# Sixteen projection blocks of a hybrid decoder layer as eight pairs of seven products each, with x of the SSD kept in memory by chunks

## The chip, the core and the metric

The kernel runs on one core of one Trainium2 chip. A core has a matrix engine (TensorE, PE), a vector engine (VectorE, DVE), a scalar engine (ScalarE, ACT), GpSimd (POOL) and a queue engine (SyncE, SP), and 16 DMA engines that all queues share. TensorE writes to PSUM (eight banks of 128 x 512 float32). The metric is the device time of one execution, in microseconds (us).

## The reference

One decoder layer over 1024 tokens of width 1024, in float32: a Mamba-2 scan (SSD) and a differential attention side by side, merged by gates, then a gated convolutional FFN. Cut to what the change touches:

```python
mod = silu(c) @ w_ada + b_ada                    # six rows of 1024: sh1, sc1, g1, sh2, sc2, g2
h = rms_norm(x, pre_norm1_w) * (1 + sc1) + sh1
z, xbc, dt_raw, q, k, v, gates = split(h @ w_in) # 1024, 1536, 16, 1024, 1024, 1024, 2048
xbc = silu(causal_dwconv(xbc, conv_w, conv_b))   # four taps
xs, B, C = split(xbc)                            # 1024, 256, 256
y_ssd = ssd(xs, dt, A, B, C)                     # chunks of 128 tokens; times silu(z), norm
q, k = partial_rope(q), partial_rope(k)          # 16 heads of 64, the first 16 dims of a head turn
merged = sigmoid(gate_ssd) * (y_ssd @ w_ssd_o) + sigmoid(gate_att) * (y_att @ w_attn_o)
x = x + g1 * rms_norm(merged @ w_out)
u = causal_dwconv(h2 @ w_up, ...)                # h2 from x, sh2, sc2
x = x + g2 * rms_norm((gelu(u_gate) * u_val) @ w_down)
```

## The kernel before

**Products in three parts.** A float32 operand is split into a high part, rounded to the fast matmul's precision, and the rest, low (`split`, lines 92 to 94: ScalarE makes hi, VectorE lo). A product is hi·hi + hi·lo + lo·hi (`mm3`, lines 112 to 117). A *block* is 128 columns of a weight against all tokens: two halves of 512 tokens, eight k tiles of 128, three matmuls each, so 48 matmuls of 128x512 (`block_half`). h is held transposed and split in `hT[k][half]`, k the tile of 128 channels.

**Storage.** Working tiles of 128 x 1024 float32 come from a list of slots (`SL.get`, `SL.put`): a tile that takes a slot waits for all that still read or write the tile before it. Weights come through `wraw` (three buffers), `whi` and `wlo` (four each). In PSUM `ps_mm` has two pairs of banks, `ps_wa` two single banks, `ps_wb` and `ps_wc` one each.

**Order.** Each engine works through one list in order. In a `tc.manual_schedule` stretch the engines named run in the order of the program; elsewhere, and for the others, a planner orders them by its own estimates. POOL's list is always the planner's. SP issues the loads and stores, in order, and waits at each for what it needs.

**Stages**, by TensorE:

1. x is normed, scaled and transposed; beside it the first gate block and xbc blocks 0 and 1.
2. Gate block 1, xbc blocks 2 to 11, gate block 2. After each xbc block comes its convolution, one ScalarE step and three on VectorE (line 443) out of PSUM, then silu; the results `xbcT[0..11]` stay in slots until the SSD is done. Beside it run the *ada sums*: 32 tiles of `w_ada` (512 KB each, four buffers `adas`) are scaled by c and summed on VectorE (`ada_sum`), eight to a row; `ada_row` (lines 389 to 404) adds the partitions with two matmuls, adds b_ada (in `brow`, loaded by POOL's queue) and stores the row (`rowd`) for later stages.
3. z, in three column groups of 346 to 348, eight token tiles each, with softplus and decays of the SSD beside it. Each tile is evicted by ScalarE and VectorE (lines 585, 586) to `ev` and stored. Here POOL makes the first six *down sums* (`down_sums`, lines 409 to 420): two loads of `w_down` (512 KB each), four subtractions of 128 x 512, two stores to `wtd`, for the FFN's down projection, which uses the same scheme of seven products as the change.
4. The SSD by chunks, with v beside it.
5. Gate blocks 3 to 7, with the other five down sums on POOL.
6. q and k: four blocks with rope (lines 911 to 915, POOL has one multiplication of it, line 913) and one more of each without (`w_q`, `w_k` block 2), stored by head in pieces (`store_qk`, 16 stores a rope block); beside it y of the SSD is turned (`turn_y`).
7. so: eight blocks y @ w_ssd_o, times the gates, to memory (`msd`). At blocks 2 and 3, `load_qk` fetches q and k of the first two heads.
8. Attention by heads, in which the rest of q and k is projected; its output product; out; the up projection; down.

The up projection (lines 1452 to 1454, from 1256.9 to 1685.3 us) already computes its 44 blocks as 22 pairs of seven products.

Of the kernel before, what the change touches and what calls it, by code (L numbers as in the profile page):

```python
# [61 lines left out]
def kernel(ctx: ExitStack, tc: tile.TileContext, a: dict, out: bass.AP, dbg=None):  # L62
# [94 lines left out]
    xhs = [SL.get(f"xh{i}", F32, (P, 2, HALF)) for i in range(2)]  # L157
    vev = SL.get("vev", F32, (P, 2, HALF))
# [72 lines left out]
    def make_h(k, half):  # L231
# [4 lines left out]
        xh = xhs[n_h // 2 % 2][:, n_h % 2, :]  # L236
# [85 lines left out]
    SL.put(junk, *adat, *acc0, *xts, *xhs)  # L322
# [30 lines left out]

    def gate_out(ps, half, dst):
# [4 lines left out]
    for half in range(2):  # L359
        gate_out(pg0[half], half, gsd[0])  # L360

    def gate_block(j):
        w = load_block(a["w_gate"][j], f"wgs{j}")
        for half in range(2):
            ps = ps_wa(f"gs{j}_{half}")
            block_half(ps, w, hT, half)
            gate_out(ps, half, gsd[j])

    gate_block(1)

    accr = [SL.get(f"accr{i}") for i in range(2)]
    adas = [SL.get(f"adas{i}") for i in range(4)]
    nrow = SL.get("nrow")

    def ada_load(u):
        r, k = divmod(u, KD)
        SP.dma_start(adas[u % 4], a["w_ada"][k * P : (k + 1) * P, (r + 2) * D : (r + 3) * D])

    def ada_sum(u):
        r, k = divmod(u, KD)
        acc = accr[r % 2]
        if k == 0:
            V.tensor_scalar(acc, adas[u % 4], scl[:, 0:1], None, op0=ALU.mult)
        else:
            V.scalar_tensor_tensor(acc, adas[u % 4], scl[:, k : k + 1], acc, op0=ALU.mult, op1=ALU.add)

    def ada_row(r):
        g, acc = r + 2, accr[r % 2]  # L390
        br, nr = brow[0:1, :], nrow[0:1, :]
        G.dma_start(br, a["b_ada"][0:1, g * D : (g + 1) * D])
        if g != 3:
            G.dma_start(nr, a["norms"][r : r + 1, :])
        for half in range(2):
            pr = (ps_wb, ps_wc)[half](f"adar{g}_{half}")
            hsl = slice(half * HALF, (half + 1) * HALF)
            T.matmul(pr, ones, acc[:, hsl], start=True, stop=True)
            V.tensor_tensor(br[:, hsl], pr[0:1, :], br[:, hsl], op=ALU.add)
        if g != 3:  # L400
            V.scalar_tensor_tensor(br, br, 1.0 if g == 4 else 0.0, nr, op0=ALU.add, op1=ALU.mult)
        if r == 0:
            V.tensor_scalar(br, br, 0.5, None, op0=ALU.mult)
        G.dma_start(rowd[r], br)

    brow = SL.get("brow")
# [14 lines left out]

    n_ada, rows_done = 0, 0


    cu = [SL.get(f"cu{i}") for i in range(2)]
    xbcT = []
    with tc.manual_schedule(engines={EN.PE}):
        for b in range(12):
            if b < 2:
                ps = px0[b]  # L430
                for u in (2 * b, 2 * b + 1):
                    ada_load(u)
            else:
                w = load_block(a["w_xbc"][b], f"wx{b}")
                ps = ps_mm(f"xbc{b}")
                for half in range(2):
                    block_half(ps[:, half, :], w, hT, half)
            pf = ps.rearrange("p h t -> p (h t)")
            u = cu[b % 2]
            cw = vec[:, V_CW + 4 * b : V_CW + 4 * b + 4]  # L440
            A.activation(u, pf, AF.Identity, scale=cw[:, 3:4], bias=vec[:, V_CB + b : V_CB + b + 1])
            for d in (1, 2, 3):
                V.scalar_tensor_tensor(u[:, d:], pf[:, : S - d], cw[:, 3 - d : 4 - d], u[:, d:], op0=ALU.mult, op1=ALU.add)
            o = SL.get(f"xbcT{b}")
            A.activation(o, u, AF.Silu)
            xbcT.append(o)
            if b >= 2:
                while rows_done < n_ada // KD:
                    ada_row(rows_done)
                    rows_done += 1  # L450
                for _ in range(4 if b in (5, 9) else 3):
                    ada_sum(n_ada)
                    if n_ada + 4 < 32:
                        ada_load(n_ada + 4)
                    n_ada += 1
        gate_block(2)
    ada_row(3)
    assert n_ada == 32 and rows_done == 3
    SL.put(*cu, *accr, *adas, nrow, brow)
    wdr = [SL.get_last(f"wdr{i}", F32, (P, 2, HALF)) for i in range(2)]  # L460
    wds = [SL.get_last(f"wds{i}", F32, (P, 2, HALF)) for i in range(2)]
    xsT, BT, CT = xbcT[:8], xbcT[8:10], xbcT[10:12]
    if dbg is not None and "xbcT" in dbg:
        for b in range(12):
            SP.dma_start(dbg["xbcT"][b], xbcT[b])
# [90 lines left out]
    with tc.manual_schedule(engines={EN.PE, EN.DVE, EN.Activation, EN.SP}):  # L556
        for t_, (c0, wdt) in enumerate(thirds):
            if t_ == 0:
                wz = []
                for kp in range(4):  # L560
                    wz.append(split_z(c0, wdt, kp, z_raw.pop(0)))
            else:
                wz = wz_next
# [1471 lines left out]
```

## Time and profile before

| | |
|---|---|
| median of 3 runs | 1907.18 us (1906.95 to 1908.35) |
| the profiled execution | 1905.24 us, its span 1903.5 us |
| granted TensorE clock | 0.999 |
| TensorE busy | 1860.1 us, 98% of the span |
| VectorE, ScalarE, POOL busy | 1205.6, 848.8, 213.0 us |
| moved by DMA | 309.48 MB, 163 GB/s in the mean |

A line of a group shows source line, engine, operation, output<-input, shapes and count, then busy time and mean ns of one, then the idle time of the engine ahead of it and what ended that. In the table by windows each row is a stretch of time with the busy time of each engine in it. L115 is line 115 of the kernel before; the kernel after has other line numbers.

### The profile page before, as it was taken

To read this page: it belongs to the slowest core of one execution; us is meant where nothing else is said; L and a number is where in the kernel's file an instruction comes from. 1 tells how busy PE (TensorE), PEld (TensorE's weight loads), DVE (VectorE), ACT (ScalarE), POOL (GpSimd) and SP (SyncE) were. 2 spreads that over 40 slices of the span, in tenths; PEclk is the share of its full clock that TensorE was granted. 3 is DMA by queue.
4 is the path that set the end of the run, shared out by engine and by line. 5 is a ranking of instruction groups with operands and counts; after the bars stand their busy time and mean duration, and the time that the engine had idled before them with its cause. 6 is when DMAs were issued, how large, how long until landed. Compare 5 with 4: busy or idle time off the path is not lost.

```text
span 1903.5 us, 24513 instructions
## 1 busy us (share of the span) xinstructions
PE 1860.1 (98%) x9128; PEld 1552.4 (82%) x9128; DVE 1205.6 (63%) x1815; ACT 848.8 (45%) x1628; POOL 213.0 (11%) x225
## 2 busy tenths in 40 slices
PE   6999999999999999999999999999999999999998
PEld 4788898888888888888888788888788888888886
DVE  6957344575235237767667465378888888876545
ACT  5522124464223115665656423465454545455532
POOL 0000253453351000000000010000000000000001
PEclk9999999999999999999999999999999999999999
DMA  9834374233766846565652666122323322378754
GB/s 306 268 115 152 129 246 153 72 117 128 257 198 146 265 153 181 150 189 159 164 164 84 218 221 219 45 78 89 127 100 108 114 100 94 108 224 302 249 152 159
DMA packets 135575, 309.48 MB, mean 163 GB/s; under 512 B 17056, under 2 KB 48416, under 8 KB 135456
## 3 DMA queue, kind: packets, MB, share of 16 engines
q1 hardware_dynamic: 127808, 281.65, 46.3%
q0 software_dynamic: 7648, 26.26, 4.0%
q8 instruction: 72, 1.18, 0.3%
q14 instruction: 47, 0.39, 0.1%
HBM read 218.97 MB, written 88.88 MB: 162 GB/s over the span
## 4 chain that ended last, share of the span: by engine, by line
PE 77%; DVE 9%; DMA 5%; ACT 5%; POOL 2%; issue 2%; SPq 1%; POOLq 0%; ACTq 0%; DVEq 0%
PE upx L1453 3%; PE upx L1452 3%; PE upx L1454 3%; PE o L1143 3%; PE xbc L115 2%; PE xbc L116 2%; PE xbc L117 2%; DMA wdr<-in_w_down 2%; PE dx L1816 2%; PE dx L1817 2%; PE dx L1815 2%; PE dy L1816 2%; PE dy L1817 2%; PE dy L1815 2%; PE v L667 2%
## 5 line engine op out<-in xcount | busy, mean ns | idle before, releaser
L1452 PE MATMUL upx<-t,wu_t 128*128 128x512 f32 x264 | 103.6, 392 | 1.8 <-DVE cv L1878 1.0
L1453 PE MATMUL upx<-t,wu_t 128*128 128x512 f32 x264 | 102.9, 390 | 0.2 <-DVE t L1570 0.2
L1454 PE MATMUL upx<-t,wu_t 128*128 128x512 f32 x264 | 102.8, 389 | 0.0
L1426 ACT ACTIVATE wu_t<-sab 128x512 fp32r<-128x512 f32 x57 | 34.2, 627 | 133.1 <-DVE sab L1443 133.1
L1131 ACT COPY aT<-at 128x512 f32<-128x512 f32 (+2 forms) x96 | 46.1, 480 | 102.8 <-PE at L1130 102.8
L1143 PEld LDWEIGHTS o<-vt,aT 128*128 128x128 f32 x576 | 74.6, 191 | 9.8 <-ACT aT L1131 5.8
L1143 PE MATMUL o<-vt,aT 128*128 128x128 f32 x576 | 80.9, 277 | 0.3
L94 DVE TENSOR_TENSOR g_lo<-gst,g_hi 128x1024 fp32r<-128x1024 f32 (+1 forms) x42 | 47.5, 1135 | 49.6 <-ACT g_hi L93 49.5
L142 POOL TENSOR_TENSOR rsf<-rsf,nhalf 128x1 f32<-128x1 f32 x8 | 5.6, 705 | 628.9 <-DVE rsf L141 626.1
L93 ACT ACTIVATE g_hi<-gst 128x1024 fp32r<-128x1024 f32 (+1 forms) x42 | 41.4, 988 | 64.3 <-DMA gst<-gld_s 35.3
L142 POOL TENSOR_TENSOR sqt<-sqt,nhalf 128x4 f32<-128x4 f32 x16 | 16.6, 1036 | 465.3 <-DVE sqt L141 465.3
L1104 DVE TENSOR_REDUCE nmx<-sc 128x1 f32<-128x640 f32 (+3 forms) x64 | 65.6, 1025 | 2.2
L1084 PE MATMUL sc<-kst,qst 128*128 128x512 f32 (+2 forms) x192 | 63.8, 340 | 0.0
L115 PE MATMUL xbc<-hT,wx_hi 128*128 128x512 f32 x160 | 63.5, 397 | 0.0
L1085 PE MATMUL sc<-klo,qst 128*128 128x512 f32 (+2 forms) x192 | 63.2, 346 | 0.0
L117 PE MATMUL xbc<-hT,wx_lo 128*128 128x512 f32 x160 | 62.3, 389 | 0.0
L116 PE MATMUL xbc<-hT,wx_hi 128*128 128x512 f32 x160 | 62.2, 389 | 0.0
L115 PE MATMUL z<-wz_hi,hT 128*128 128x346 f32 (+1 forms) x192 | 62.1, 323 | 0.0
L116 PE MATMUL z<-wz_lo,hT 128*128 128x346 f32 (+1 forms) x192 | 61.7, 322 | 0.0
L117 PE MATMUL z<-wz_hi,hT 128*128 128x346 f32 (+1 forms) x192 | 61.4, 320 | 0.0
L1452 PEld LDWEIGHTS upx<-t,wu_t 128*128 128x128 f32 x264 | 49.5, 188 | 14.5 <-DVE cv L1878 3.2
L1470 DVE SCALAR_TENSOR_TENSOR ug<-cg,vec,ug 128x1023 f32<-128x1023 f32 (+1 forms) x44 | 56.3, 1280 | 7.7 <-ACT ug L1469 6.7
(451 smaller groups left out, 5840.6 us busy)
## 6 DMA issues: line engine op xcount, KB each, us to landing
adas<-in_w_ada SPq DMA_DIRECT2D x32, 512.0 KB, 4.9
wdr<-in_w_down POOLq DMA_DIRECT2D x22, 512.0 KB, 6.8
wtd<-wds POOLq DMA_DIRECT2D x22, 512.0 KB, 4.3
wuf<-in_w_up SPq DMA_DIRECT2D x22, 512.0 KB, 3.5
gld_s<-gsum SPq DMA_DIRECT2D x22, 512.0 KB, 2.8
gst<-gld_s SPq DMA_DIRECT2D x20, 512.0 KB, 4.5
wdt_raw<-wtd SPq DMA_DIRECT2D x20, 512.0 KB, 4.8
wuv<-in_w_up SPq DMA_DIRECT2D x19, 512.0 KB, 3.5
```

The lines of the kernel that those rows point to most:

```text
L115: T.matmul(ps, lh, rh, start=(i == 0), stop=False)
L116: T.matmul(ps, lh, rl, start=False, stop=False)
L117: T.matmul(ps, ll, rh, start=False, stop=(i == n - 1))
L1084: T.matmul(sc[:, n0:n1], qs_[s][:, tsl], ks_[s][:, n0:n1], start=True, stop=False)
L1104: V.reduce_max(nmx[:, bq, s : s + 1], sc[:, :L], axis=AX.X, negate=True)
L1143: T.matmul(po_of[j, grp][:, qi, :], at[:, k, :], vt[j % 2][:, kt, :], start=(kt == 0), stop=(kt == i))
L1452: T.matmul(out_, wh, xh_, start=(k == 0 and first), stop=False, skip_group_check=not first)
L1453: T.matmul(out_, wh, xl_, start=False, stop=False, skip_group_check=not first)
L1454: T.matmul(out_, wl, xh_, start=False, stop=(k == end), skip_group_check=not first)
L1815: T.matmul(o, gh[:, kk, tsl], wh, start=(k == 0 and not more), stop=False, skip_group_check=more)
L1816: T.matmul(o, gh[:, kk, tsl], wl, start=False, stop=False, skip_group_check=more)
L1817: T.matmul(o, gl[:, kk, tsl], wh, start=False, stop=(k == KF - 1), skip_group_check=more)
```

## The change

Sixteen blocks are computed in pairs: gate blocks 4 with 5 and 6 with 7, block 2 of w_q with block 2 of w_k, and xbc blocks 2 with 3 to 10 with 11. Channels of h and tokens are each cut in half, so that h is a 2 by 2 matrix of quarters (b11, b12, b21, b22) and the two blocks' weights another; Strassen's scheme in Winograd's form gives the four results in seven products of half the depth (12 matmuls each) instead of eight. It takes four sums of quarters of h (t1 to t4, made once, split into hi and lo) and four sums of weights for each pair (`x_sum`), and the seven products are summed in three banks: X three times, Z and Y.

- Gate blocks 1 to 3 come first, as plain blocks; beside them VectorE and ScalarE make t1 to t4 from h in 32 bits (`hr`). The quarter b12 of `hT` goes to memory (`h12d`), gives up its slots, and is loaded again during the last pair.
- The eight pairs follow, in an order written by hand for all engines but POOL. `post` does what belongs to a pair's blocks (tanh and store, scale and store, convolution and silu) under the products of the next pair, out of SBUF (`cg`, `cv`) instead of PSUM.
- PSUM is laid out anew for pairs and z: four single banks (`ps_x`), X and Z of a pair in two of them by turns, Y in `ps_wa`.
- Ada sums: six in each of the pairs 2 and 3, four in pair 4, with two buffers; the other 16 in z, one a tile from tile 6 on, with four. The rows are finished at z's tiles 2, 5, 16 and 23.
- xbc blocks 0 to 7 (x of the SSD) are stored to memory by chunks (`xcd`) and loaded a chunk at a time, two ahead (`xch`), instead of staying in slots.
- The stage of gates 3 to 7 and the two q, k blocks without rope are gone; the four rope blocks share one pair of `hi`, `lo` tiles, and `turn_y` follows them four at a time. The five down sums of the gates' stage are at so's blocks 0 to 4, and `load_qk` of the first two heads at blocks 5 and 6.

```diff
+    order = (("b11", "X"), ("b21", "Z"), ("t2", "X"), ("t1", "Y"), ("t3", "X"), ("b22", "Y"), ("t4", "X"))
+    pairs = [("gs", 4, 5), ("gs", 6, 7), ("qk", 2, 2)] + [("xbc", b, b + 1) for b in range(2, 12, 2)]
...
+    def x_mms(m, p):
+        n, bk = order[p]
+        o, t = xbank[m][bk], xhl[m, p]
+        first = p in (0, 1, 3)
+        for k in range(KH):
+            wh, wl = t[:, 0, k, :], t[:, 1, k, :]
+            xh_, xl_ = HX[n][k][:, 0, :], HX[n][k][:, 1, :]
+            T.matmul(o, wh, xh_, start=(k == 0 and first), stop=False, skip_group_check=not first)
+            T.matmul(o, wh, xl_, start=False, stop=False, skip_group_check=not first)
+            T.matmul(o, wl, xh_, start=False, stop=(k == KH - 1), skip_group_check=not first)
...
+            for p in range(7):
+                if p == 3:
+                    bank["Y"] = ps_wa(f"xy{m}")
+                x_mms(m, p)
+                if p == 0:
+                    if m > 0:
+                        x_sum(m, 3)
+                    x_ahead(m, 3)
+                    if m > 0:
+                        A.copy(cgv[(m - 1) % 2][1][:, :HALF], xbank[m - 1]["X"])
+                elif p == 1:
+                    A.copy(ev_[:, 0, :], bank["X"])
...
+                elif p == 5:
+                    V.tensor_tensor(cv[:, HALF:], bank["X"], ev_[:, 0, :], op=ALU.add)
+                    x_sum(m + 1, 0)
+                    x_ahead(m, 8)
...
+                for st in steps_at[before].get(p, ()):
+                    post(m - 1, st)
+                if m in (1, 2) and p < 6 or m == 3 and p in (1, 3, 4, 5):
+                    ada_sum(m < 3 or p < 4)
...
+                    if p == 2:
+                        for k in range(KH):
+                            hT[k][1] = new_hl(f"b12_{k}")
+                            SP.dma_start(hT[k][1].rearrange("p h t -> p (h t)").bitcast(F32), h12d[k])
...
 # z, tile nz = 8 * t_ + i
+                if nz < 6:
+                    post(last_pair, nz)
+                if nz < 22:
+                    if nz >= 2 and n_ald < 20:
+                        ada_load()
+                    if nz >= 6:
+                        ada_sum()
+                if nz in (0, 3, 14, 18):
+                    row_load((0, 3, 14, 18).index(nz))
+                if nz in (2, 5, 16, 23):
+                    ada_row((2, 5, 16, 23).index(nz))
...
 # SSD
-            T.transpose(px[:, j * P : (j + 1) * P], xsT[4 * g + j][:, tok], ident)
+            T.transpose(px[:, j * P : (j + 1) * P], xch[c % 2][:, 4 * g + j, :], ident)
+        if g == 1 and c < 6:
+            SP.dma_start(xch[c % 2], xcd[:, c + 2])
...
-    for j in range(3, 8):
-        down_sums(n_dn)
-        n_dn += 1
-        w = load_block(a["w_gate"][j], f"wgs{j}")
-        ps = ps_mm(f"gs{j}")
...
 # so, block j
-            if j in (2, 3):
-                s = j - 2
+            if j < 5:
+                down_sums(n_dn)
+                n_dn += 1
+            elif j == 5:
+                SL.put(*wdr, *wds)
+                qst, kst, klo = [[[SL.get(f"{n}0_{s}", F32R) for s in range(2)]] for n in ("qst", "kst", "klo")]
+            if j in (5, 6):
+                s = j - 5
                 load_qk(s, qst[0][s], kst[0][s], klo[0][s])
```

More of the change, by code (lines that the diff above doesn't have):

```diff
@@ L377, in ada_load @@
[L377 to L394, printed above, removed]
-        for half in range(2):
[L396 to L404, printed above, removed]
@@ new lines, with x_load @@
+    xw, xhl, xbank = {}, {}, {}
+    x_loads = [(n, m) for m in range(len(pairs)) for n in "fv"]
+    def x_load():
+        if not x_loads:
+            return
+        n, m = x_loads.pop(0)
+        kind, i, j = pairs[m]
+        src = {"gs": ("w_gate", "w_gate"), "xbc": ("w_xbc", "w_xbc"), "qk": ("w_q", "w_k")}[kind]["fv".index(n)]
+        t = xw[n, m] = wp.tile([P, 2, KH, P], F32, tag="wraw", name=f"xw{n}{m}", bufs=3)
+        SP.dma_start(t.rearrange("p h k c -> p (h k c)"), a[src][(i, j)["fv".index(n)]])
@@ L420, in down_sums @@
             G.dma_start(wtd[("12", "34")[i]][:, k, :, :], wds[i])
[L422 to L465, printed above, removed]
     sm1 = SL.get("sm1", F32, (P, 8, 8, NH))
@@ L891 @@
     load_y(0)
-    qscale = {"w_q": 0.125, "w_k": 1.0}
     ropc = SL.get("ropc")
@@ L896 @@
     SP.dma_start(rops, a["rops"])
-    thl = [[SL.get(f"th{n}{i}", F32R) for n in ("hi", "lo")] for i in range(2)]
+    hi, lo = [SL.get(f"th{n}", F32R) for n in ("hi", "lo")]
     qf = SL.get("qf")
```

387 lines of the change are left out of this document (303 added, 84 removed).

## The prediction

> **What bounds the kernel now.** I read the page first, then the windows by stage, then the waits of each stage that the change touches, and last the order of the instructions on each engine in the two built programs.
>
> ```profile
> span 1903.5 us, 24513 instructions
> PE 1860.1 (98%) x9128; PEld 1552.4 (82%) x9128; DVE 1205.6 (63%) x1815; ACT 848.8 (45%) x1628; POOL 213.0 (11%) x225
> ```
> ```profile
> 88.30:214.80 126.50, 126.50 (x546) 102.14 (x545) 82.59 (x74) 34.76 (x35) 3.89 (x8) 1.00 0.38 123
> 214.80:307.60 92.80, 92.80 (x590) 92.42 (x589) 36.21 (x76) 21.28 (x42) 43.94 (x49) 1.00 0.69 236
> 487.00:540.00 53.00, 53.00 (x235) 43.89 (x234) 6.95 (x5) 10.17 (x15) 25.05 (x27) 1.00 0.73 258
> 601.40:693.50 92.10, 91.91 (x420) 75.12 (x419) 25.69 (x34) 14.97 (x19) 0.00 (x0) 1.00 0.69 221
> ```
>
> The columns of a window are its length, then the busy time of PE, PEld, DVE, ACT and POOL, the granted clock, the DMA share and GB/s. TensorE has no gap in xbc with gate 2 (first row), z (second), gates 3 to 7 (third) and the SSD output product, so (fourth). A matmul that goes is a gain, and a wait that comes is a loss in full. POOL was busy beside z and gates 3 to 7, and idle beside so. There the change moves things.
>
> **The products removed.** Eight pairs of blocks take 7 products of 12 matmuls, where two plain blocks take 96: 12 fewer a pair, 96 in all. Their price is the distance of starts, read where the same scheme runs already (the up projection), first and last of 16 starts:
>
> ```profile
> 1681.65 0.39 PE L1454 MATMUL upy<-b,wu_b 128*128 128x512 f32 x1
> ...
> 1685.05 0.39 PE L1454 MATMUL upx<-t,wu_t 128*128 128x512 f32 x1
> ```
>
> (1685.05 − 1681.65) / 15 = 0.227 us, so 96 of them are **−21.8 us**. A product is 2.72 us, a pair 19.0, a plain block of 48 is 10.9.
>
> **Do pairs run dense?** The up projection says nearly:
>
> ```profile
> 1256.90:1685.28 428.38, 425.08 (x1882) 349.50 (x1880) 361.40 (x480) 219.58 (x330) 1.47 (x2) 1.00 0.31 108
> L1452 PE MATMUL upx<-t,wu_t 128*128 128x512 f32 x264 | 103.6, 392 | 1.8 <-DVE cv L1878 1.0
> L1452 PE MATMUL upy<-b,wu_b 128*128 128x512 f32 x88 | 34.5, 392 | 1.3 <-ACT evs L1875 1.3
> ```
> ```profile
> L1878 DVE TENSOR_TENSOR cv<-upx,evs x20: 681/684/692, 1315.5 to 1681.0; 128x512 f32<-128x512 f32 x20
> L1470 DVE SCALAR_TENSOR_TENSOR ug<-cg,vec,ug 128x1023 f32<-128x1023 f32 (+1 forms) x44 | 56.3, 1280 | 7.7 <-ACT ug L1469 6.7
> ```
>
> Its 22 pairs waited 1.8 + 1.3 us, 0.14 a pair: eight pairs **+1.1**. VectorE has in an xbc pair what it has there, 14 steps of 0.684 and 6 convolution steps of 1.28: 17.3 of 19.0 us.
>
> In pairs 2 and 3 six, in pair 4 four ada sums take the convolutions' place or come on top, and each waits for its own load, with two buffers for four:
>
> ```profile
> adas<-in_w_ada SPq DMA_DIRECT2D x32, 512.0 KB, 4.9
> L387 DVE SCALAR_TENSOR_TENSOR accr<-adas,scl,accr 128x1024 f32<-128x1024 f32 x20 | 25.6, 1281 | 2.2 <-DMA adas<-in_w_ada 1.9
> ```
>
> A buffer is needed again two products (5.4 us) after the sum that frees it began; less 1.3 for that sum some 4.1 us are left, and the products' 0.7 or so of slack on VectorE. A load that lands in 4.9 costs nothing; six loads, two of weights and two stores in 19.0 us are 10 × 0.524 MB, 275 GB/s against 123 there now, so one of 6 us is likely and costs about 1.4 a pair, since the evacuations of the banks stand behind the waiting sum. I take **+2.0** (0 to 6).
>
> At the end of the last pair z's first tile takes the bank that ScalarE must still copy out, one copy with its signals:
>
> ```profile
> L1859 ACT COPY cv<-upx x19: 564/568/589, 1322.0 to 1666.7; 128x512 f32<-128x512 f32 x19
> ```
>
> **+0.8.** The tile's last weights and the reloaded quarter of h land before it by my count (0 to 3).
>
> **Z: a row that waits behind three down sums.** This is the largest unknown. The program order is that the second row of ada (b_ada, line 788 after) is loaded at tile 3 and added on VectorE at tile 5. In the built program POOL has that load behind the first TENSOR_TENSOR of the fourth down sum, and VectorE, in order, has the row's addition ahead of the eviction of tile 6 and of all four lo halves that tile 8 needs. So PE stops at tile 8 until POOL has got through three sums and a load.
>
> ```profile
> 225.57 1.28 POOL L415 TENSOR_TENSOR wds<-wdr 128x512 f32<-128x512 f32 x1 [5.25 <-DMA zd<-ev]
> ...
> 253.04 1.28 POOL L416 TENSOR_TENSOR wds<-wdr,wds 128x512 f32<-128x512 f32 x1 [1.01 <-DMA wdr<-in_w_down]
> ...
> 292.79 1.29 POOL L415 TENSOR_TENSOR wds<-wdr 128x512 f32<-128x512 f32 x1 [6.38 <-DMA wdr<-in_w_down]
> ```
> ```profile
> wdr<-in_w_down POOLq DMA_DIRECT2D x12, 512.0 KB, 7.2
> wtd<-wds POOLq DMA_DIRECT2D x12, 512.0 KB, 4.4
> DMA to landing us min/median/max: 3.8/7.2/8.5
> brow<-in_b_ada POOLq DMA_DIRECT2D x4, 4.0 KB, 3.7
> L586 DVE SCALAR_TENSOR_TENSOR ev<-ev,z 128x346 f32<-128x346 f32 x8 | 4.1, 513 | 11.1 <-ACT ev L585 7.0 <-DMA zd<-ev 4.0
> L94 DVE TENSOR_TENSOR wz_lo<-wz_raw,wz_hi 128x692 fp32r<-128x692 f32 x3 | 2.6, 880 | 0.7 <-ACT wz_hi L93 0.5
> L399 DVE TENSOR_TENSOR brow<-adar,brow x8: 668/669/672, 135.5 to 215.7; 1x512 f32<-1x512 f32 x8
> ```
>
> A sum takes POOL (292.79 − 225.57) / 5 = 13.4 us from start to start. Count from the end of the last pair. The first sum's second wdr load waits for the sixth weight split of that pair, about −9.5; with 0.5 to issue, 7.2 to land and three steps of 1.29 the sum ends at +2.1. The second ends 13.4 + 1.0 later (the row's two small loads are issued in it), the third another 13.4: 29.9. Two stores, a load and a store issued (about 1.6), 7.2 to land, 1.3 for the step: 39.5 or so; the row's load lands 3.7 later, 43.2. VectorE then has two additions (1.3), the eviction of tile 6 (0.7 with its dt part), an ada term (0.7 to 1.3) and the first lo half (0.9): 46.8. Tile 8 is due at 0.8 + 8 × 92.8/24 plus two ada rows on PE, each (126.5 − 11 × 10.9) / 4 = 1.7: 35.2. The stall is **+11.6**. With each of the four loads at 3.8 it is 0, at 8.5 it is 17.
>
> That DVE and POOL hold each other up is in the rows of the same stage:
>
> ```profile
> L505 DVE TENSOR_TENSOR sm<-sm,sm 128x128 f32<-128x128 f32 x6 | 1.8, 292 | 0.2
> L497 DVE TENSOR_TENSOR sm<-sm,sm 128x128 f32<-128x128 f32 x1 | 1.3, 1332 | 0.0
> ```
>
> The same form takes 0.29 us, and 1.33 where it started at 253.15 beside POOL's step above. The change brings 6 convolution steps and 16 ada sums into this stage. VectorE has 36.2 + 22 × 1.28 + three more rows (about 7), 71 us of 92.8, and by the measured 1.04 for each of POOL's 24 steps at most 25 more, which it can still hold. I add **+0.5** for the split at tile 15. The Trainium skill, SBUF — State Buffer, Who interferes with whom, says that a VectorE instruction with two SBUF inputs and a GpSimd instruction that reads SBUF block each other for a whole instruction; the trace agrees (1.33 against 0.29), and it speaks against moving two-input work beside the down sums.
>
> The granted clock is 1.00 in every window above. The Trainium skill, TensorE: Matmul & The Clock Gate, Why this matters for your kernels, lets the clock fall to half after idle gaps of some 3 us; by it the stall would cost, as an estimate, 2 us more. No stretch here shows that.
>
> The last ada row stands ahead of half of v's lo halves on VectorE: two additions and one step of 1.2, up to 2.5 us at the start of the SSD, where x comes from memory two chunks ahead and should not be late. **+1.0** (0 to 2.5).
>
> **Gates 3 to 7 and q2, k2 gone; five down sums into so.** The gates ran dense, so only the saving counted above is in them. They also hid five down sums:
>
> ```profile
> 511.22 1.30 POOL L415 TENSOR_TENSOR wds<-wdr 128x512 f32<-128x512 f32 x1 [8.04 <-DMA wdr<-in_w_down]
> ...
> 536.64 1.28 POOL L415 TENSOR_TENSOR wds<-wdr 128x512 f32<-128x512 f32 x1 [5.54 <-DMA wdr<-in_w_down]
> ```
> ```profile
> 599.77 0.42 SPq L864 DMA_DIRECT2D khd<-thhi  x1
> ...
> 602.09 0.42 SPq L865 DMA_DIRECT2D kld<-thlo  x1
> L912 DVE STREAM_SHUFFLE sw<-qf 128x1024 f32<-128x1024 f32 x4 | 5.3, 1334 | 0.0
> L914 DVE TENSOR_TENSOR sw<-sw,rops 128x1024 f32<-128x1024 f32 x4 | 10.3, 2570 | 0.0
> L915 DVE TENSOR_TENSOR qf<-qf,sw 128x1024 f32<-128x1024 f32 x4 | 4.9, 1217 | 8.1 <-POOL qf L913 8.0
> L93 ACT ACTIVATE wso_hi<-wso_raw 128x1024 fp32r<-128x1024 f32 x8 | 8.5, 1056 | 48.8 <-DMA wso_raw<-in_w_ssd_o 48.8
> L94 DVE TENSOR_TENSOR wso_lo<-wso_raw,wso_hi 128x1024 fp32r<-128x1024 f32 x8 | 9.8, 1223 | 21.2 <-ACT wso_hi L93 21.2
> wso_raw<-in_w_ssd_o SPq DMA_DIRECT2D x6, 512.0 KB, 5.0
> klo<-kld SPq DMA_DIRECT2D x4, 256.0 KB, 9.0
> ```
>
> Times now from the start of so: 4.7 us of turning y (92.1 − 8 × 10.9), then blocks of 10.9. q2 and k2 used to lie between the last rope block and so. Now the fourth rope block's steps stand on VectorE behind so's first eviction (15.6 + 0.7): shuffle, multiply, add, hi, lo, 1.3 + 2.6 + 1.2 + 1.1 + 1.2, to 23.7. Its 16 stores leave SP 0.46 apart, 7.4 us, and three more issues come before the load of block 3's weights is out at 32.5: landed 37.5, hi and lo 39.8, due 37.4. **+2.7** with the eviction's load beside it (0 to 5).
>
> POOL's first sum there needs the slots of those stores, so its second load starts at about 33.5: landed 40.5, done 44.4. Four more at 12.9 (between the 12.7 of the rows above and 13.4) end at 96. SP, in order, has the loads of k's low half for the heads 0 in slots that the last sum frees, and so waits from about 80 to 96; behind it stand the other loads of the first two heads, two stores, v and the weights of w_k3. The last of k low needs the store of the sum (96 + 4.4) and 9.0 to land: 110. PE ends so at 94.6, has q products of later heads to fill in (14 groups of three matmuls, 9.5 us), 104, and waits **+6.0**. A sum ending at 90 costs nothing; each us later costs about one.
>
> **The sum.** −21.8 + 1.1 + 2.0 + 0.8 + 11.6 + 0.5 + 1.0 + 2.7 + 6.0 = +3.9. The profiled execution took 1905.24 (span 1903.5 and 1.74 outside it), 1.94 less than the median of 1907.18: its like would be 1909.1, and the median **1911**. 0.2%, about what a measurement can tell from no change, is 3.8 us.
>
> **The rivals.** *POOL's period is short* (faster). Both stalls hang on how long a down sum takes. At 11 us each, as where loads land in 5, the row comes two periods of 2.4 and two loads of 2.2 sooner, 9 us, and the last sum of so ends at 86: −9 and −6, 1911 − 15 = 1896; at 12 us about 1902. For it: the two periods in gates 3 to 7 were 12.7, and z's loads landed in as little as 3.8. Against: DMA has more to carry in the new z (16 ada loads). Periods half a microsecond shorter than I take make 4 us, that is, before and after alike.
>
> *POOL's period is long* (slower). Z's 236 GB/s are 21.9 MB in 92.8 us; 16 ada loads of 0.524 make them 326 GB/s, and five sums with four such transfers each take so from 221 to 335. If a sum then takes 16 us, the two periods ahead of the row add 5 and the four in so add 12: 1911 + 17 = 1928. For it: these rates, and the lock on VectorE; against: POOL's loads have a queue of their own.
>
> *All waits hidden:* −21.8 + 1.1 + 0.8 + 0.5 + 1.0 leaves 1889. It needs POOL to run the row's load earlier than its order says.
>
> **Chances.** Forecast case (1903 to 1919) 0.45, short period 0.22, long period 0.26, all hidden 0.07. Below 1892 lies the hidden case and a little of the short one, above 1925 half of the long one: range 1892 to 1925. Faster than before by over 0.2%: hidden, most of the short case, a fifth of the forecast, 0.33; within 0.2%: 0.18; slower 0.49.
>
> **What would show it.** In the profile after: PE waits at z's tile 8 for a lo half, and behind it VectorE waits for brow from a DMA about 17 us (right), or neither (the sum then falls below before). SP waits for POOL ahead of klo at so's end, and PE for sc or w_k. Pairs of 19.0 to 19.5 us; if they take over 20 with VectorE waiting on adas, the load term was too small. A span under 1895 would make the row's wait wrong, one over 1925 the periods.

## The result, and the profile after

| | before | after |
|---|---|---|
| median | 1907.07 us (1904.55 to 1908.35, 4 runs) | 1948.50 us (1946.34 to 1950.14, 4 runs) |
| ratio | | 1.0218, 95% interval 1.0201 to 1.0236 |
| profiled execution, span | 1905.24, 1903.5 us | 1950.14, 1948.3 us |
| granted TensorE clock | 0.999 | 0.986 |

The kernel became 41 us slower, where 4 were predicted. The direction held, though the prediction gave "slower" no more than 0.49; the size did not, and it lies above the range. The head of the page of the kernel after:

```profile
span 1948.3 us, 24577 instructions
PE 1856.3 (95%) x9032; PEld 1541.4 (79%) x9032; DVE 1280.5 (66%) x1943; ACT 890.7 (46%) x1716; POOL 218.3 (11%) x225
```

The 96 matmuls are gone (9128 to 9032). TensorE was busy for 98% of the span before and is for 95% after. The windows by stage of the kernel after (pairs; z; SSD, v and rope; so; attention up to the first output product), and under them attention before, show where (columns as in the prediction: length, busy PE, PEld, DVE, ACT, POOL, clock, DMA share, GB/s):

```profile
108.90:285.00 176.10, 159.76 (x673) 127.32 (x671) 129.13 (x157) 78.09 (x117) 12.32 (x11) 0.97 0.53 174
285.00:400.60 115.60, 104.76 (x605) 99.26 (x606) 70.26 (x107) 26.20 (x48) 41.32 (x48) 0.96 0.73 249
400.60:619.90 219.30, 216.09 (x1164) 176.23 (x1162) 134.05 (x176) 107.87 (x267) 86.68 (x69) 1.00 0.40 130
619.90:717.70 97.80, 93.72 (x417) 75.57 (x416) 31.39 (x36) 15.93 (x19) 33.23 (x36) 0.98 0.70 226
717.70:1122.80 405.10, 382.09 (x2177) 323.74 (x2176) 261.26 (x537) 223.15 (x596) 21.21 (x21) 0.97 0.59 170
```
```profile
693.50:1078.50 385.00, 377.79 (x2177) 321.20 (x2176) 260.23 (x535) 222.11 (x594) 16.57 (x16) 1.00 0.56 158
```

| term | predicted | measured | from |
|---|---|---|---|
| matmuls removed | −21.8 | −21.8 | 96 x 0.227 |
| pair stage | +3.9 | +23.7 | 176.1 − 8 x 19.05 |
| z | +12.1 | +17.7 | 115.6 − 92.8 − three more ada rows of 1.7 |
| SSD, v, rope | +1.0 | +0.3 | 219.3 − (179.4 + 61.4 − two blocks of 10.9) |
| so | +2.7 | +5.7 | 97.8 − 92.1 |
| attention | +6.0 | +20.1 | 405.1 − 385.0 |
| sum | +3.9 | +45.7 | the span grew by 44.8 |

Later stages are as long as before (825.5 and 825.0 us). Three places carry the miss: the pairs, z, and so with attention.

**Pairs.** Timelines of three engines in one xbc pair (start, us, engine, line; in brackets the idle time ahead and what ended it):

```profile
226.33 0.50 PE L458 MATMUL xx<-xt,xw_t 128*128 128x512 f32 x1 [0.43 <-ACT xevs L657]
233.03 0.50 PE L458 MATMUL xx<-xt,xw_t 128*128 128x512 f32 x1 [0.96 <-DVE xcv L663]
```
```profile
223.38 1.28 DVE L516 SCALAR_TENSOR_TENSOR xbcT<-xcg,vec,xbcT 128x1021 f32<-128x1021 f32 x1
226.84 0.69 DVE L434 TENSOR_TENSOR xw_t<-xwv,xw_t 128x512 fp32r<-128x512 f32 x1 [2.19 <-ACT xw_t L433]
...
229.78 2.60 DVE L516 SCALAR_TENSOR_TENSOR xbcT<-xcv,vec,xbcT 128x1022 f32<-128x1022 f32 x2
232.29 0.68 DVE L663 TENSOR_TENSOR xcv<-xx,xevs 128x512 f32<-128x512 f32 x1
```
```profile
224.75 1.06 ACT L518 ACTIVATE xbcT<-xbcT 128x1024 f32<-128x1024 f32 x1 [3.88 <-DVE xbcT L516]
225.72 0.57 ACT L657 COPY xevs<-xx 128x512 f32<-128x512 f32 x1
226.18 0.63 ACT L433 ACTIVATE xw_t<-xwv 128x512 fp32r<-128x512 f32 x1
```

ScalarE stands 3.88 us at the SiLU (L518) for VectorE's third convolution step. Only behind it comes the copy (L657) that frees bank X for the next product. VectorE idles 2.19 us for the high part that is late for the same reason, then does two convolution steps (2.60) ahead of the addition (L663) that frees X again. Each pair has these two waits, 0.43 and 0.96 us of idle TensorE, and its period is 21.0 us, not 19.05. In pair 8 the second one is long:

```profile
279.62 0.79 PE L458 MATMUL xx<-xt,xw_t 128*128 128x512 f32 x1 [5.52 <-DVE xcv L663]
```
```profile
270.01 6.22 DVE L516 SCALAR_TENSOR_TENSOR xbcT<-xcv,vec,xbcT 128x1023 f32<-128x1023 f32 x3 [0.44 <-ACT xbcT L514]
278.08 0.88 DVE L94 TENSOR_TENSOR wz_lo<-wz_raw,wz_hi 128x692 fp32r<-128x692 f32 x1 [1.85 <-ACT wz_hi L93]
278.88 0.68 DVE L663 TENSOR_TENSOR xcv<-xx,xevs 128x512 f32<-128x512 f32 x1
```

Three convolution steps take 6.22 us instead of 3 x 1.28 (POOL's first down sum runs beside them; what it adds is measured below), and a low part of z's weights, which waits for ScalarE behind its SiLU, stands ahead of the addition. In pairs 2 to 5 VectorE also waited for ada loads: a row of the waits of this stage (total, times, longest), and the stall that followed, with two of the next matmuls:

```profile
DVE accr L482 <- DMA adas<-in_w_ada: 10.6, 7, 3.7
```
```profile
196.99 0.50 PE L458 MATMUL xx<-xt,xw_t 128*128 128x512 f32 x1 [2.01 <-ACT xevs L649]
...
198.50 0.63 PE L460 MATMUL xx<-xt,xw_t 128*128 128x512 f32 x1
198.93 0.63 PE L458 MATMUL xx<-xt,xw_t 128*128 128x512 f32 x1
```

The matmuls behind the stall start 0.43 us apart instead of 0.227, and the granted clock there is 0.50: the clock is at half.

**Z.** TensorE, VectorE, POOL and SP at the two long stalls, tile 8 and tile 16:

```profile
322.16 0.43 PE L115 MATMUL z<-wz_hi,hT 128*128 128x346 f32 x1 [3.07 <-ACT wz_hi L93]
...
362.76 0.66 PE L115 MATMUL z<-wz_hi,hT 128*128 128x348 f32 x1 [5.49 <-ACT wz_hi L93]
```
```profile
319.54 1.28 DVE L799 TENSOR_TENSOR brow<-adar,brow 1x512 f32<-1x512 f32 x2 [7.02 <-DMA brow<-in_b_ada]
...
350.42 0.52 DVE L836 SCALAR_TENSOR_TENSOR ev<-ev,z 128x346 f32<-128x346 f32 x1 [7.00 <-DMA zd<-ev]
```
```profile
316.25 0.52 POOL L788 DMA_DIRECT2D brow<-in_b_ada  x1
```
```profile
322.66 0.33 SPq L471 DMA_DIRECT2D adas<-in_w_ada  x1
330.10 0.37 SPq L1603 DMA_DIRECT2D sh2c<-rowd  x1
```

Tile 8 is the forecast stall: VectorE waits for a row whose load POOL issued in its fourth down sum. Tile 16 was not forecast: VectorE waits 7.00 us for the store of an eviction. And SP stands from 323.0 to 330.1 at the load of sh2c, a column of a stored row, which the planner had put there although the program has it behind attention.

**So and attention.** POOL's last subtraction, SP's loads and TensorE's stalls:

```profile
719.99 1.29 POOL L703 TENSOR_TENSOR wds<-wdr,wds 128x512 f32<-128x512 f32 x1
```
```profile
690.71 0.54 SPq L1234 DMA_DIRECT2D w_q_raw<-in_w_q  x1
721.30 1.08 SPq L1110 DMA_DIRECT2D klo<-kld  x2
...
730.05 9.85 SPq L1300 DMA_DIRECT2D vt<-vd  x8
740.00 0.38 SPq L1234 DMA_DIRECT2D w_k_raw<-in_w_k  x1
```
```profile
736.89 0.45 PE L1321 MATMUL sc<-kst,qst 128*128 128x128 f32 x1 [8.65 <-DMA kst<-khd]
...
747.00 0.80 PE L1275 MATMUL w_kp<-hT,w_k_hi 128*128 128x512 f32 x1 [5.20 <-DVE tqlo L1256]
```

SP is blocked at k low, as forecast, but from 71 to 101 us after so's start, not from 80 to 96. The weights of w_k3, behind eight issues of v that took 9.85 us, make a second stall.

### The profile page after: what moved, and what is told of

It is laid out like the page before. It is cut to its first block, busy times and chain, and to the rows that moved or that the text cites. A ratio compares the mean times of both kernels' runs of the same rounds, so it can differ in the third digit from the quotient of the medians.

```text
span 1948.3 us, 24577 instructions
## 1 busy us (share of the span) xinstructions
PE 1856.3 (95%) x9032; PEld 1541.4 (79%) x9032; DVE 1280.5 (66%) x1943; ACT 890.7 (46%) x1716; POOL 218.3 (11%) x225
## 4 chain that ended last, share of the span: by engine, by line
PE 63%; DVE 13%; DMA 10%; ACT 7%; issue 3%; POOL 3%; SPq 2%; POOLq 0%; ACTq 0%; DVEq 0%
DMA wdr<-in_w_down 3%; PE upx L1689 3%; PE upx L1688 3%; PE upx L1690 3%; PE o L1380 3%; DMA adas<-in_w_ada 2%; PE dx L2052 2%; PE dx L2053 2%; PE dx L2051 2%; PE v L938 2%; PE dy L2053 2%; PE dy L2051 2%; PE dy L2052 2%; PE v L940 2%; PE v L939 2%
## 5 line engine op out<-in xcount | busy, mean ns | idle before, releaser
L1688 PEld LDWEIGHTS upx<-t,wu_t 128*128 128x128 f32 x264 | 49.5, 188 | 14.8 <-DVE cv L2114 3.5
L1689 PEld LDWEIGHTS upx<-t,wu_t 128*128 128x128 f32 x264 | 49.6, 188 | 10.6 <-DVE t L1806 0.5
L115 PE MATMUL z<-wz_hi,hT 128*128 128x346 f32 (+1 forms) x144 | 49.1, 341 | 9.2 <-ACT wz_hi L93 8.6
L1690 PEld LDWEIGHTS upx<-t,wu_t 128*128 128x128 f32 x264 | 49.6, 188 | 10.3
L1706 DVE SCALAR_TENSOR_TENSOR uv<-cv,vec,uv 128x1023 f32<-128x1023 f32 (+1 forms) x44 | 56.2, 1277 | 1.3 <-ACT uv L1705 1.3
L1666 DVE TENSOR_TENSOR wu_t<-sab,wu_t 128x512 fp32r<-128x512 f32 x57 | 39.3, 689 | 26.6 <-ACT wu_t L1662 26.6
L458 PE MATMUL xx<-xt,xw_t 128*128 128x512 f32 x96 | 40.2, 419 | 15.7 <-DVE xcv L663 11.2
```

The source lines that it names most:

```text
L115: T.matmul(ps, lh, rh, start=(i == 0), stop=False)
L1688: T.matmul(out_, wh, xh_, start=(k == 0 and first), stop=False, skip_group_check=not first)
L1689: T.matmul(out_, wh, xl_, start=False, stop=False, skip_group_check=not first)
L1690: T.matmul(out_, wl, xh_, start=False, stop=(k == end), skip_group_check=not first)
L1706: V.scalar_tensor_tensor(u[:, d:], c_[:, : S - d], fw[:, 2 - d : 3 - d], u[:, d:], op0=ALU.mult, op1=ALU.add)
```

## The experiments

Medians are compared with the changed kernel's 1948.50; a ratio is that to the kernel before in the same set of runs. Times of single stages and stalls are those of the profiled execution of each run.

**Order inside the pairs** (e1_order).

```diff
-            if d == 3: A.activation(u, u, AF.Silu) ...      # in post(), p = 2 and p = 4
+                if p in (3, 6): silu(m - 1, p // 3 - 1)     # behind the copy of X
-    "xbc": {0: (0,), 1: (1,), 2: (2,), 3: (3,), 4: (4, 5)}
+    "xbc": {0: (0,), 1: (1,), 2: (2,), 3: (3,), 4: (4,), 5: (5,)}
```

> The changed kernel with another order inside the xbc pairs only: the SiLU of a block's three convolution steps stands behind the copy that frees bank X instead of ahead of it, and the sixth convolution step stands behind the addition that frees X instead of ahead of it. Theory 1 (order): the two waits a pair, 0.6 and 1.1 us beyond the pace, come from this order alone. The xbc pairs then go from 21.0 to 19.1-19.4 us, the pair stage from 176.1 to 162-167 us (ada waits of pairs 2 to 4 stay), the whole from 1948.5 to 1935-1939. In the last pair the stall of 5.9 us goes to under 1.5 as well. Rival A (load): VectorE has 17.3 of 19.0 us of work in a pair and is late on average; pairs stay at 20.5-21, the time within 3 us of 1948.5. Rival B (POOL): the last pair's stall is POOL's down sum slowing VectorE's steps; then it stays above 3 us whatever the order.

1948.37 us, ratio 1.0218 (1.0200 to 1.0236): nothing gained in the median of four runs between 1944.85 and 1952.34. Pairs 6 and 7 went from 21.0 to 20.24 us, where 19.1 to 19.4 were expected, and pair 8 from 28.1 to 22.2. Its SiLU's store blocks SP longer, the first ada load left at 130.8 instead of 128.1, and pair 2 took 28.5 instead of 21.0. The pair stage kept 4.7 us of gain. In z the stall at tile 8 grew from 3.07 to 9.04 us, for its row still came when POOL's sums let it, and the one at tile 16 fell from 5.49 to 0.75 and, one matmul on, 1.49:

```profile
322.82 0.65 PE L115 MATMUL z<-wz_hi,hT 128*128 128x346 f32 x1 [9.04 <-ACT wz_hi L93]
```

Z as a whole took 1.5 us of the gain back, and the profiled execution kept 3 us, which the medians do not show. So the run did not isolate the order.

It does not decide rival B either: the last stall fell to 0.53 us, but POOL's subtractions came later, beside one of the three convolution steps (2.27 us; the others 1.28). The other runs with the old order divide that stall. Where POOL's first sum began behind the three steps (e2, e3, e6, e13, e14), these took 1.28 us each and the stall was 3.2 us; where they met (the changed kernel, e4, e5, e10, e12), it was 5.5 us. So POOL's part is 2.3 us and the order's 3.2. VectorE and TensorE of e14 (under "All at once"), against the 6.22 and 5.52 above:

```profile
261.71 3.92 DVE L516 SCALAR_TENSOR_TENSOR xbcT<-xcv,vec,xbcT 128x1023 f32<-128x1023 f32 x3 [0.44 <-ACT xbcT L514]
269.02 0.79 PE L458 MATMUL xx<-xt,xw_t 128*128 128x512 f32 x1 [3.22 <-DVE xcv L664]
```

**Early rows** (e2_rows), **16 ada sums in the SSD** (e3_ssd), **late columns** (e5_cols), **rows and columns** (e6_rowscols).

```diff
-        G.dma_start(brow[0:1, :], a["b_ada"]...)             # row_load(r) at tiles 0, 3, 14, 18
+        G.dma_start(brow[32 * r : 32 * r + 1, :], a["b_ada"]...)   # e2: all rows, during pair 4
-                        ada_load() ... ada_sum()             # z, tiles 2 to 21
+            ada_sum()                                        # e3: once per half chunk u of the SSD
-        SP.dma_start(t, rowd[r]...)                          # sh2c, a2c: where the planner likes
+        SP.dma_start(t, rowd[r]...)                          # e5: in SP's fixed order, at so's start
```

> The changed kernel with the four rows of b_ada and three of norms loaded in one go by POOL ahead of its first down sum, on partitions 0, 32, 64 and 96, so that no row's load stands behind a down sum. Theory 2 (row behind sums): tile 8's stall in z (3.07 + 0.89 us and about 2 us of half clock) goes, z takes 109-111 instead of 115.6 us, the time is 5-6 us lower, and the 5.5 us at tile 16 stay. Rival A: tile 8 was late because its weights or the evictions were, the row was only beside it: z stays above 113. Rival B: tile 16's stall too comes from rows on POOL: z falls to 103-105.

> As the kernel with early rows, and the last 16 ada loads and sums and two of the rows moved out of z into the SSD, one sum a half chunk. Theory 3 (DMA): tile 16's stall comes from z's evictions, whose two buffers wait 7.0 and 3.0 us for their stores behind 16 ada loads of 0.5 MB; with the loads gone z takes 94-97 us, and the SSD 3.4 us (two rows) to 8 us more; the time is 12-18 us below the changed kernel's. Rival A: the stall comes from VectorE's convolution steps and POOL's sums, which stay; z then stays above 102. Rival B: the SSD has no room on VectorE beside POOL and grows by over 10 us, so that the time falls by less than 8.

> The changed kernel with one edit: the loads of two columns of the modulation (sh2c and a2c, from the rows 1 and 2 in memory) are issued at the start of so; until now the scheduler has put them on SP in the middle of z, where they wait for POOL's stores of the rows. Theory 5 (SP's order): these two loads hold up SP in z (7.4 us from 322.7 to 330.1 in the changed kernel), so that the stores of z's evictions, the ada loads and the third group of weights behind them are late. Then tile 16's stall (5.5 us) falls below 2 us and z from 115.6 to 106-111 us; tile 8's stays, since its row still waits for POOL; the time is 4-9 us lower. Rival (DMA): the stores and loads are late because the DMA engines are 0.73 busy there; z stays above 113.

> The early rows and the late columns together. Theory 5: each edit alone leaves the other head of a queue waiting; together both stalls of z go, z takes 95-101 us, the time is 13-20 us below the changed kernel's. Rival (DMA): with the 16 ada loads still in z the evictions' stores stay late, z stays above 106.

| | median | ratio (95%) | z, us | stalls at tile 8, between, at tile 16 |
|---|---|---|---|---|
| after | 1948.50 | 1.0218 (1.0201 to 1.0236) | 115.6 | 3.07, 1.01, 5.49 |
| e2, rows | 1950.65 | 1.0231 (1.0215 to 1.0247) | 119.7 | none, 2.42 + 7.63, 3.17 |
| e5, columns | 1946.32 | 1.0207 (1.0190 to 1.0224) | 114.9 | 3.81, 0.66, 4.11 |
| e6, both | 1943.05 | 1.0195 (1.0179 to 1.0210) | 111.3 | none, none, 7.66 |
| e3, rows, ada out | 1942.66 | 1.0188 (1.0173 to 1.0203) | 103.2 | none, none, 3.70 |

Taken away alone, no cause was worth much: theory 2 held for tile 8 and failed for the time, and theory 5 failed as the single cause of tile 16, with z on its rival's side of 113. In e3 z fell by 12, of which the SSD took 6.2 back. Its 103.2 lies above theory 3's 97 and on rival A's side of 102; the trace shows SP's block behind the stall that is left, and with that block gone too, and other edits beside, z takes 96.6 (e7, below). SP and VectorE of e3:

```profile
314.69 0.32 SPq L835 DMA_DIRECT2D zd<-ev  x1
329.41 0.37 SPq L1600 DMA_DIRECT2D sh2c<-rowd  x1
```
```profile
335.60 0.52 DVE L834 SCALAR_TENSOR_TENSOR ev<-ev,z 128x346 f32<-128x346 f32 x1 [9.55 <-DMA zd<-ev]
```

In e6, without that block but with the 16 loads, z stayed above 106, as its rival said, and VectorE still waits for stores. Its DMA issues in z (median us to landing last) and VectorE:

```profile
adas<-in_w_ada SPq DMA_DIRECT2D x16, 512.0 KB, 6.3
zd<-ev SPq DMA_DIRECT2D x8, 173.0 KB, 7.1
```
```profile
340.23 0.52 DVE L835 SCALAR_TENSOR_TENSOR ev<-ev,z 128x346 f32<-128x346 f32 x1 [6.35 <-DMA zd<-ev]
```

**Loads or VectorE in z** (e13_noloads), on e6. It leaves out 12 of the 16 tiles of `w_ada` that z sums, so its modulation rows are not the layer's.

```diff
-                    if nz >= 2 and n_ald < 20: ada_load()
+                    if 2 <= nz < 6: ada_load()               # the 16 sums stay
```

> As the kernel with early rows and late columns, but of the 16 ada loads in z only four are made; the 16 sums stay and run on those four (12 loads are left out). It tells the transfers apart from VectorE's work. Theory (transfers: stores of the evictions stand behind the loads): the 7.7 us stall at tile 16 falls below 2 us, z from 111 to 96-100 us. Rival (VectorE: 16 sums beside six convolution steps and POOL): z stays above 106. Between them both have a part.

1929.21 us, 1.0123 (1.0108 to 1.0139); z 100.1 us, no stall over 0.4. The rival fell. Its stores land in

```profile
zd<-ev SPq DMA_DIRECT2D x8, 173.0 KB, 4.8
```

So the third layer in z is these 12 loads, not VectorE's work, with the stores of 173 KB (tiles 8 to 15) behind them and two `ev` buffers. The run does not say by which way they act. They share the DMA engines with these stores, which land 7.1 us after their issue in e6 and 4.8 here. They also make SP stand: a load waits at SP until VectorE has summed its buffer, and the next store stands behind it. SP's wait for that in z of e6 (total, times, longest):

```profile
SPq L471 <- DVE accr L482: 12.0, 6, 5.0
```

**Down sums out of so, and so's order** (e4_sums, e10_so).

```diff
+                if nz == 23: down_sums(n_dn); n_dn += 1      # e4: seven in z
-            if j < 5: down_sums(n_dn)
+            if j < 4: down_sums(n_dn)
-            load_qk(0 and 1) at j = 5, 6, slots in part those of the sums
+            load_qk(0) at j = 4, free slots; load_qk(1) and v behind block 7    # e10
```

> The changed kernel with seven down sums in z and four in so instead of six and five. Theory 4: attention starts late because SP stands at the last sum's slot (721.3) with k low, v and w_k3 behind it; with the sum ending 14 us earlier that wait goes: first scores follow the q products without a stall of over 2 us, so to first ao shrinks from 405 to 386-393 us, the time by 12-18 us. Rival A: the loads would be late anyway, because the queue or the DMA engines (0.70 busy) carry too much there: it shrinks by under 6 us. Rival B: the seventh sum in z delays a row and with it z or the SSD's start by as much as is gained.

> The changed kernel with one edit: in so the loads of head 0 use the three slots that the down sums do not hold, and those of head 1 and v stand at the end of SP's order, behind the first weights of q and k. Five sums stay in so. Theory: of the 20 us that attention lost, the part behind SP's blocked issue (v, w_k3: 5.2 us and the half clock after it) goes, while the wait for head 1 behind the last sum stays: attention 405 -> 393-400 us, time 5-12 us lower. Rival: the sums' end alone decides; then nothing changes (within 3 us).

e4: 1944.88 us, 1.0199 (1.0182 to 1.0216); from so's start to the first output product 497.6 us, after 502.9, before 476.9. Z grew by 3.2 us with its seventh sum, as rival B had it in part. The sums ended 14 us sooner after so's start, and the planner then put the first weights of q behind k low and v:

```profile
732.81 0.80 PE L1278 MATMUL w_qp<-hT,w_q_hi 128*128 128x512 f32 x1 [12.65 <-ACT w_q_hi L1252]
```

e10: 1946.01 us, 1.0209 (1.0191 to 1.0226), 500.0 us. The wait for w_k3 is gone; head 1, still behind the fifth sum, takes its place, as its rival said:

```profile
737.77 0.45 PE L1325 MATMUL sc<-kst,qst 128*128 128x128 f32 x1 [11.60 <-DMA kst<-khd]
```

**Ada's buffers** (e12_ada4).

```diff
+                adas += [SL.get(f"adas{i}") for i in (2, 3)]  # pair 2; two again in pair 4
+                if m == 0 and p in (3, 4): ada_load()         # the first two, in pair 1
```

> The changed kernel with one edit: the ada sums beside pairs 2 to 4 have four buffers instead of two and their first two loads stand one pair earlier. Theory (two buffers hold VectorE up in pairs 2 to 5): the pairs' periods 20.97, 19.56, 19.04 go to 19.04-19.2, the fifth from 25.5 to 21.0 like the other xbc pairs, the pair stage from 176.1 to 168.5-171; the rest is as it was, the time 4-7 us lower. Rival (loads are late because DMA or SP is): the sums still wait over 1 us each and the stage stays above 173.

1938.72 us, 1.0172 (1.0156 to 1.0187): pairs 2 to 4 at 19.04 us each, pair 5 20.6 instead of 25.5, the stage 169.5. Two buffers cost 6.6 us there, 4.9 of it in pair 5. The time fell by 9.8, more than the 4 to 7 expected.

**All at once** (e7_all, e8_late, e9_best, e11_best, e14_noorder). All have early rows and late columns, and all but e14 the new order in the pairs, with the SiLUs one product later than in e1 (p = 4 and 6). "First ao" is the first output product of attention. e9 loads two tiles of `w_ada` over two others that are not summed yet, so its rows are not the layer's; e11 is e9 with these loads issued later.

| | ada sums | down sums in z, so | median | ratio (95%) | pairs | z | SSD to rope | so to first ao |
|---|---|---|---|---|---|---|---|---|
| e7 | 16 pairs (two buffers), 16 SSD | 8, 3 | 1918.87 | 1.0065 (1.0050 to 1.0080) | 164.4 | 96.6 | 228.2 | 495.1 |
| e8 | 16 z, 16 SSD | 8, 3 | 1926.49 | 1.0110 (1.0091 to 1.0129) | 153.2 | 103.5 | 240.1 | 492.9 |
| e9 | 16 pairs (four), 16 SSD | 7, 4, so's order of e10 | 1899.40 | 0.9962 (0.9949 to 0.9975) | 153.2 | 96.6 | 227.3 | 489.2 |
| e11 | as e9 | as e9 | 1898.24 | 0.9956 (0.9944 to 0.9969) | 153.2 | 96.7 | 225.1 | 488.9 |
| e14 | as e11, old order in the pairs | as e11 | 1912.97 | 1.0033 (1.0020 to 1.0046) | 167.2 | 97.6 | 226.0 | 488.6 |

> Early rows, late columns, the last 16 ada sums in the SSD, eight down sums in z and three in so, and the SiLUs of a pair one step later (behind the copy of bank Y) with the sixth convolution step behind the addition; 16 ada sums stay in the pairs. If each place has the cause given so far: xbc pairs of 19.1-19.3 us, the pair stage 163-168 (ada waits stay), z 95-99, the SSD 6 us longer, so to first ao 482-488 instead of 503; the time 1905-1916. Rival (one bound for all, DMA or POOL, that only moves): the sum of the stages stays within 10 us of the changed kernel's, above 1935.

> As the kernel before it, but no ada sum in the pairs: the first 16 in z with four buffers, the other 16 in the SSD. Theory (ada loads with two buffers hold up pairs 2 to 5): pair stage 154-158 us, z 97-103 us with the loads back; the time 1898-1910. Rival A: the pairs without ada still take over 162, then the loads were not what held them. Rival B: z with 16 loads takes over 106.

> All edits together in a new division: 16 ada sums in pairs 2 to 4 with four buffers instead of two and the first two loads one pair earlier, none in z, 16 in the SSD; early rows, late columns, the pairs' order; seven down sums in z and four in so, whose slots the first head's loads no longer take, and head 1's loads and v last on SP. Theory (every stall has its own head of a queue, and the DMA engines only bound z with the ada loads in it): pairs 153-157 us, z 96-99, SSD 185-188, from so's start to the first ao 478-488; the time 1890-1904, below the kernel before. Rival (one bound that moves): the gains again show up as waits elsewhere, and the time stays above 1910.

> As the kernel with all edits (e9_best), with the loads of ada terms 14 and 15 issued two sums later, after the sums that free their buffers (there they overwrote terms 12 and 13 before these were summed). Theory: the time does not depend on it, 1896-1903 us, 0.2 to 0.5% below the kernel before; pairs 153-154, z 96-98 us. Rival: the two later loads stall pair 4 as with two buffers, then the pair stage is over 156 us.

> As the best kernel (e11_best), but with the changed kernel's order in the pairs (SiLU ahead of the copies, conv steps five and six ahead of the addition). It prices that order by itself. Theory: xbc pairs of 21.0 us again, the last with its stall, the pair stage 153 -> 164-168 us, the time 8-14 us above 1898. Rival (later stages take the loss up, as they took up gains before): the stage grows but the time by under 4 us.

e9 and e11 met the times expected; e7 and e8 came out above theirs. In e8 all eight pairs run at 19.04 us (the last with 0.8 more for z's first bank), but the time is higher than e7's: the ada loads are back beside z, POOL's eighth sum ends at 377, and the tile `xtk`, into which ScalarE copies the SSD's first x, has a slot of it. ScalarE and TensorE of e8:

```profile
383.41 0.59 ACT L987 COPY xtk<-px 128x512 f32<-128x512 f32 x1 [8.63 <-DMA wtd<-wds]
384.54 1.11 PE L982 MATMUL px<-ident,xch 128*128 128x128 f32 x4 [14.11 <-DVE sm L989]
```

e14 prices the order: 14.0 us in the pair stage, 14.7 in the time, a little above the 8 to 14 expected; here nothing later took it up, so its rival fell. e11 is 50 us faster than the changed kernel and 0.4% faster than the kernel before (interval of the ratio 0.9944 to 0.9969). Its windows (pairs, z, SSD to rope, so, attention):

```profile
108.60:261.80 153.20, 152.52 (x674) 125.95 (x673) 126.41 (x157) 78.51 (x117) 6.50 (x10) 1.00 0.55 186
261.80:358.50 96.70, 96.41 (x596) 93.95 (x597) 48.80 (x85) 25.02 (x47) 51.15 (x56) 1.00 0.73 257
358.50:583.60 225.10, 220.48 (x1172) 177.57 (x1170) 157.20 (x198) 108.82 (x270) 100.17 (x70) 1.00 0.50 162
583.60:681.40 97.80, 94.37 (x420) 76.32 (x419) 35.05 (x40) 17.09 (x21) 26.70 (x28) 0.98 0.78 252
681.40:1072.50 391.10, 379.58 (x2173) 322.30 (x2172) 259.40 (x534) 222.06 (x594) 21.08 (x21) 0.99 0.57 163
```

What is left of the 21.8 us is 8: so and attention keep 12 us more than before, and the stage from the SSD to rope is 6 longer than in the changed kernel, 3.4 of it two ada rows that z no longer has.

## Why the prediction was wrong

- **The matmuls removed: right.** With nothing in their way eight pairs take 153.2 us (e8, e11), the 152.4 of the working and the 0.8 for z's first bank.
- **"Do pairs run dense?": the step that failed most.** It compared VectorE's load, 17.3 of 19.0 us, with the up projection's, and took its waits. The load was not what held the pairs up (VectorE is as busy in e11's pair stage, 126.4 us, and TensorE has no stall there). What decides is the order within a product. The prediction said that the up projection has the same six convolution steps; its blocks have two each, xbc's three, and the third and the SiLU behind it stand ahead of the copies. 1.1 was forecast, 14.0 measured (e14). POOL's sum beside the last pair cost 2.3 more (e12 against e14); the prediction looked for that lock in z alone. With the 6.6 of ada and the 0.8 of the bank this makes the 23.7 of the stage.
- **Ada in the pairs:** right mechanism, 2.0 forecast (0 to 6), 6.6 measured (e12). Loads landed in 4.8 us in the median, as taken; the last one took 6.5, VectorE waited 3.7 us for it, and that one late sum moved all after it in pair 5 (4.9 of the 6.6).
- **Z, the row behind three down sums:** shown (e2), 11.6 forecast, some 5.5 measured with its half clock (3.07 + 0.89 + 1.5), because the last pair itself took 28.1 us while POOL's sums went on, so that tile 8 was due later. The working then stopped at the first stall. It listed each queue that a row's load passes on POOL, and not the loads that read the stored rows on SP; and it priced DMA's higher rate through POOL's period alone, not through the stores of the evictions. Taking away one or two of the three left the others (e2, e5, e6); taking all away gave 96.6 (e7). The working's count has a slip of 0.5 us (29.9 + 1.6 + 7.2 + 1.3 is 40.0, not 39.5), which changes nothing here.
- **Rope into so:** 2.7 forecast for block 3; it was 2.24 + 0.53 us and 1.6 of half clock, and rope's first wait (1.31) the rest of 5.7 for the most part.
- **So's sums into attention:** right place, 6.0 forecast, 20.1 measured. Of the terms, the sums' end was 5 us late (the first sum ended 2 us later than counted, and the four periods took 54.9 us, not 51.6), w_k3 behind v 5.2 more, the half clock 2.2; the rest is the first two heads' loads, of which 8.65 us show as one wait. e4, e10 and e11 shorten it without removing it, so how little it can be with sums in so stays open.
- **The clock: taken as 0, and wrong.** Seven stretches after stalls ran at half clock. Counted by the spacing of starts (0.43 against 0.227, 0.29 against 0.157) they cost some 10 us of the 41, 0.8 to 2.0 each; the prediction named 2 us for a stall and left them out of its sum. The Trainium skill, TensorE: Matmul & The Clock Gate, Why this matters for your kernels, asks for no idle gaps of TensorE over some 3 us, since the clock goes back to half after them. The trace agrees for the five stalls from 3.07 to 8.65 us, and it shows the half clock after two shorter ones too, 2.01 and 2.24 us.
- **Rivals:** "POOL's period is long" came nearest (1928): the period in z was 15.0 us in the mean from 269.4 to 344.4, against 13.4 taken and 16 in the rival. But it put the loss at tile 8, whose stall came out shorter than forecast, and knew nothing of the pairs' order, so part of that nearness is luck. "All waits hidden" was no part of this order of work, but most of it could be had (e11: 1898).

## What to carry to other kernels

An engine's load in a stage says whether a schedule can fit; whether it does is read from the order, step by step, at the instructions that free a bank or a buffer: put those first on every queue. Before moving work, list every reader of what it makes and every queue where that reader stands in order, also where a planner may put it early. When a stall is removed and the time stays, look for the next head of a queue in the same place before the theory is dropped: here edits that alone moved the time by −2.2 to +2.2 us (e1, e2, e5) belong to a set that together took 50 (e11).

## What the runs showed of the hardware

- In the traces of this case each of the 45 TensorE stalls of 3.2 us and more was followed by a granted clock of 0.5 (stalls within the first 60 and the last 20 us left aside). Among shorter ones it goes both ways: it followed one of 1.84 us (e4) and one of 1.86 (e13), and not one of 2.86 (e8) and one of 3.18 (e13). In the changed kernel it set in up to 2.1 us after the restart (tile 8 of z), and starts stayed apart for up to 4.4 us (tile 16).
- VectorE and POOL lengthened each other: three convolution steps took 6.22 us beside POOL's subtractions and 3.92 without (e14), and a POOL subtraction beside them 2.25 instead of 1.29, as in this row of the changed kernel:

```profile
272.90 2.25 POOL L702 TENSOR_TENSOR wds<-wdr,wdr 128x512 f32<-128x512 f32 x1
```

- A mean DMA share says little about landing: z ran dense at 0.73 (e11, without ada loads in it) and stalled at 0.73 (the changed kernel).
